# Where the residual input of a decoder layer is turned: on TensorE inside the output projection, or by VectorE's block transposes early, kept in DRAM

## The chip, the cores and the metric

The kernel runs on one core of a Trainium2 chip. The metric is the device time of one execution in microseconds (us). Before the change it is 1391.66 us, the median of 3 runs (1391.24 to 1391.66). A single execution was also taken with the hardware profiler; every number of the trace below is from that one.

## The reference

One layer of a hybrid decoder is computed for 1024 prompt tokens and 8 sample tokens, which the kernel treats as one set of 1032 columns. The width is 1024. With the branch details left out:

```python
h = rmsnorm(x, g_attn_norm)
z = h @ w_in                       # q, k, v of both branches, output gate, merge gates
y_a = attention(...) @ w_att_out   # sliding window of 128, sinks
y_m = mlstm(...) @ w_mlstm_out     # chunkwise matrix memory
mixed = sigmoid(gate_a) * y_a + sigmoid(gate_m) * y_m
x = x + mixed @ w_out              # the residual add of this case
h2 = rmsnorm(x, g_ffn_norm)
x = x + (silu(h2 @ w_gate) * (h2 @ w_up)) @ w_down
return rmsnorm(x, g_final)         # and caches and states
```

All arrays are float32. What matters here is the line `x = x + mixed @ w_out`: the raw input `x` is needed a second time, after about two fifths of the work.

## The kernel before, in words

**Layout.** Activations live with the channel on the partition and the token along the row, in 8 blocks of 128 channels by 1032 tokens. The inputs `x_prompt` and `x_sample` are stored token by token, so the residual has to be turned from [token, channel] to [channel, token] before it can be added. Float32 products are made from a high and a low part of each operand (`split`, L230: ScalarE copies the high part, VectorE subtracts to get the low part), three matmuls for each block.

**Two runs over a list of products.** The function `run` (L334) goes through a list of jobs. The first call (L2114) has 69 of them: 4 tiles by 3 column chunks first, and 19 more tiles by 3 chunks: the input projections and the first merge gates. The second call (L2119) has one job for each of the 32 remaining tiles: 16 branch tiles (8 "wm", 8 "wa", matmuls on L1385) and 16 tiles of the output projection (`wo_tile`, L1233, matmuls on L1261). The output projection makes two passes over the 8 blocks of `w_out`: in the first pass (s = 0) for one half of the tokens, in the second (s = 1) for the other. Between the two calls the other merge gates are computed (`gates`), and after the second the feed-forward part follows.

Within a job: `before()`, the matmuls (with a step of queued side work every few matmuls), the split of the weights that are used two jobs later and the load of those used four jobs later (`next_split`, L340), the evacuation, and `after()`.

**Orders.** The instructions of TensorE, SyncE (SP) and GpSimd are kept in the order in which the program writes them. For VectorE and ScalarE, those written through `main_line` (L287) keep their order among each other. All loads and most stores are issued from SP's queue, one behind the other; a transfer whose buffer is not free yet holds up all those that are written after it. Small tiles come from a pool of 11 buffers (`T`, L109), whole activations from one of 20 (`U`, L106).

**The weights of the output projection.** In the first pass each block's high and low parts, after the split, are also stored to DRAM (`KeptSlice`, L190, 512 KB each), and in the second pass loaded from there (`AgainSlice`, L205), so they are split only once.

**The residual.** `xr_load` (L1175) loads a quarter of the channels for all tokens in rows of 1 KB; two quarters are issued in the last branch jobs (L1372), two from the residual's own steps. `residual` (L1187) is side work of the output projection's first pass. For each of 8 channel blocks it transposes 8 token blocks of 128 x 128 and one of 8 tokens on TensorE (L1197, L1202) into a PSUM tile, and ScalarE copies the pieces into `X[s, th, k // 4]` (L1199, L1203), the tiles to which the evacuation adds the product (`add_half`, L1265). Side work of the same pass also splits the mixed activations of the second pass (`mix_rest`, L1218).

Of the kernel before, what the change touches and what calls it, by code (L numbers as in the profile page):

```python
# [11 lines left out]
F32 = mybir.dt.float32  # L12
# [8 lines left out]
P = 128  # L21
D = 1024
NP = 1024
NS = 8
# [19 lines left out]
LAST = (4, 5)  # L44
WARM = (22, 3, 3, 4)
START = 4
PER_A = 2.95
AHEAD = 3
LEAD = 4
# [35 lines left out]
def decoder_step(ctx, tc, x_prompt, x_sample, cache_k, cache_v, st_c, st_n, st_m, rel_bias, w_in, b_if, sinks,  # L85
# [248 lines left out]
    def run(tiles, jobs, sl, loads, splits):  # L334
        last = {}
        for n, (t, c) in enumerate(jobs):
            last[t] = n
        started = set()

        def next_split():  # L340
            main_line(splits.pop(0).split)
            if loads:
                loads.pop(0).load()

        for n, (t, c) in enumerate(jobs):
            tile_ = tiles[t]
            if t not in started:
                started.add(t)
                if tile_.before:
                    tile_.before()  # L350
            if tile_.pre:
                tile_.pre(c)
            rate = tile_.per / sum(len(rhs) for _, rhs in tile_.prods)

            def tick():
                acc[0] += rate
                if acc[0] >= 1.0 - 1e-9:
                    acc[0] -= 1.0
                    side.step(1)

            pss = []
            for i, (w, rhs) in enumerate(tile_.prods):
                if tile_.mm:
                    ps = tile_.mm(w, tick)
                else:
                    ps = ps_g(f"{w.name}_{c}")
                    gemm(ps, w.w, rhs, slice(*CHUNKS[c]), tick)
                pss.append(ps)
                if last[t] == n and splits and not w.own and not tile_.evac_first:
                    next_split()  # L370
            main_line(tile_.evac, c, *pss)
            if last[t] == n and splits and tile_.evac_first:
                next_split()
            if tile_.after:
                tile_.after()
            if n + 2 < FIRST and len(sl) > FIRST and not mark:
                sl[n + 2].split()
            if n + 1 == START and not mark:
                mark.append(len(nc.cur_bb.bb.instructions))

    def call(f, *a):
        f(*a)
        yield

    def rstd(v):
        dve.tensor_scalar(v, v, 1.0 / D, EPS, op0=ALU.mult, op1=ALU.add)
# [774 lines left out]
    X = {}  # L1161
    XG = {}
    mixed = {}
    xr = {}
    ssq = {}
    pools = {}
    R = {}
# [4 lines left out]
    def ps_d(name):  # L1172
        return pools["pd"].tile([P, 2, 512], F32, tag="d", name=name)

    def xr_load(q):  # L1175
        cols_ = slice(q * 256, (q + 1) * 256)
        for i in range(0, NB, 2):
            t = T(f"xr{i}_{q}", [P, 2, 256])
            sp.dma_start(t, x_prompt[0, i * P:(i + 2) * P, cols_].rearrange("(u p) d -> p u d", p=P))
            xr[q, i], xr[q, i + 1] = t[:, 0], t[:, 1]  # L1180
        t = T(f"xr{NB}_{q}", [P, 256])
        sp.dma_start(t[0:NS, :], x_tok[NB][:, cols_])
        xr[q, NB] = t

    PIECES = ((0, ((0, 0, 258), (1, 258, 512))), (4, ((1, 512, 516), (2, 516, 774), (3, 774, 1024))))

    def residual():  # L1187
        for k in range(KD):
            if k % 4 == 0:
                for s in range(2):  # L1190
                    for th in range(2):
                        X[s, th, k // 4] = U(f"x1_{s}{th}{k // 4}", shape=[P, 4, HB])
            q, o = k // 2, k % 2 * P
            for b0, pieces in PIECES:
                tps = ps_t(f"xr{b0}_{k}")
                for j in range(4):
                    pe.transpose(tps[:, j * P:(j + 1) * P], xr[q, b0 + j][:, o:o + P], ident)  # L1197
                for c, a, b in pieces:
                    act.copy(X[c % 2, c // 2, k // 4][:, k % 4, a - c * HB:b - c * HB], tps[:, a - b0 * P:b - b0 * P])  # L1199
                yield  # L1200
            tps = ps_t(f"xr{NB}_{k}")
            pe.transpose(tps[:, 0:NS], xr[q, NB][0:NS, o:o + P], ident[0:NS, 0:NS])  # L1202
            act.copy(X[1, 1, k // 4][:, k % 4, HB - NS:HB], tps[:, 0:NS])  # L1203
            if k in (1, 3):
                xr_load(q + 2)
            yield

    def mix_split(s, th, ks):
        for kh in range(2):
# [8 lines left out]
    def mix_rest():  # L1218
        for th in range(2):
            for k in range(0, KD, 2):  # L1220
                main_line(mix_split, 1, th, range(k, k + 2))
                yield

    d_x1 = [dp.tile([P, NT], F32, name=f"d_x1_{j}") for j in range(KD)]

    def wo_start():
        res = residual()
        side.add(itertools.islice(res, 6), mix_rest(), res)

    stage3 = ExitStack()  # L1230
    kept = {}
# [1 line left out]
    def wo_tile(s, j):  # L1233
# [5 lines left out]
        def before():  # L1239
            if s == 0 and j == 0:  # L1240
                wo_start()
                side.step(2)
            if s == 1 and j == 0:
                side.drain()
            if s == 1 and j == 1:
# [116 lines left out]
    def branch_tile(n, j):  # L1362
# [3 lines left out]
        def before():  # L1366
            if n == "m":
                mixm[j] = U(f"mixm{j}")
                if j == 0:
                    reload(back_a, d_yat, V, "yb")  # L1370
            sg_load(i + 2)
            if n == "a" and j in (5, 6):  # L1372
                xr_load(j - 5)

        def mm(w_, tick):
            rhs = ym if n == "m" else ya
# [891 lines left out]
```

## Time and profile before

| what | value |
|---|---|
| median of 3 runs | 1391.66 us |
| the profiled execution's own time | 1391.65 us |
| its span, from the first to the last instruction | 1389.9 us |
| TensorE busy | 1369.4 us, 99% of the span |
| VectorE, ScalarE, GpSimd busy | 975.4, 617.0, 242.0 us |
| mean granted TensorE clock | 0.997 |
| read from and written to DRAM | 140.31 MB, 68.96 MB |

A line of the trace names the line of the kernel, the engine, the operation, and the tiles as output<-input. "PE" is TensorE, "PEld" its weight load, "DVE" VectorE, "ACT" ScalarE, "POOL" GpSimd, "SPq" the queue that SyncE feeds. Matmuls overlap, so the time from the start of one to the start of the next is shorter than the duration shown. The DMA share of a stretch is the mean busy share of the core's 16 DMA engines.

### The profile page before, as it was taken

The page shows a single profiled execution, that of the slowest core. Times are in us where ns is not written, and L with a number is a line of the kernel's source. Part 1 is how long each engine was busy: PE and PEld are TensorE (multiplying, and loading weights), DVE is VectorE, ACT ScalarE, POOL GpSimd, SP SyncE. Part 2 cuts the span into 40 slices and gives each one's busy share as a digit, 9 for nine tenths or more (in the row PEclk, how much of TensorE's full clock was granted, in tenths as well). Part 3 has the DMA queues.
Part 4 walks back from the last instruction along what each step waited for, and adds up shares of the span by engine and source line. Part 5 has one row for each costly group of instructions (what it writes and reads, how often), then busy time and mean ns, then how long its engine had stood idle before and what let it go on. Part 6 is the DMA issues. An engine that isn't in the chain of part 4 may idle for free.

```text
span 1389.9 us, 26966 instructions
## 1 busy us (share of the span) xinstructions
PE 1369.4 (99%) x10723; PEld 1337.9 (96%) x10724; DVE 975.4 (70%) x1853; ACT 617.0 (44%) x1407; POOL 242.0 (17%) x303
## 2 busy tenths in 40 slices
PE   9999999999999999999999999999999999999996
PEld 7999889999999999999999999999999999999996
DVE  7252758886944444755587888898888878888875
ACT  6243567654443331374454343444433343333325
POOL 4012111001111100001132232333333220000003
PEclk9999999999999999999999999999999999999998
DMA  7144224114233274788423344544434468677633
GB/s 224 32 117 113 62 63 100 31 62 149 81 107 100 84 283 137 221 281 283 166 77 120 110 153 153 168 168 139 131 114 144 146 214 304 220 239 237 221 123 122
DMA packets 179173, 208.42 MB, mean 150 GB/s; under 512 B 20638, under 2 KB 137634, under 8 KB 179032
## 3 DMA queue, kind: packets, MB, share of 16 engines
q1 hardware_dynamic: 161928, 151.72, 35.1%
q0 software_dynamic: 16688, 54.40, 10.7%
q8 instruction: 84, 1.38, 0.4%
q10 hardware_dynamic: 432, 0.59, 0.1%
q14 instruction: 41, 0.34, 0.1%
HBM read 140.31 MB, written 68.96 MB: 151 GB/s over the span
## 4 chain that ended last, share of the span: by engine, by line
PE 90%; DVE 3%; ACT 2%; DMA 2%; issue 1%; POOL 0%; SPq 0%; ACTq 0%; POOLq 0%; DVEq 0%
PE af L1589 18%; PE df L1589 9%; PE ad L1589 7%; PE wo L1261 6%; PE bf L1589 5%; PE ag L1589 4%; PE dd L1589 4%; PE o L226 3%; PE mv L226 3%; PE wm L1385 3%; PE wa L1385 3%; PE q L226 3%; PE dg L1589 2%; PE bd L1589 2%; PE mk L226 2%; PE gm L226 2%
## 5 line engine op out<-in xcount | busy, mean ns | idle before, releaser
L125 POOL TENSOR_TENSOR s1f<-s1f,R 128x516 f32<-128x516 f32 x42 | 68.8, 1637 | 87.2 <-DVE s1f L125 71.5
L1589 PE MATMUL df<-Th,op6f 128*128 128x258 f32 x352 | 67.3, 283 | 1.3 <-DVE uu L125 1.3
L1589 PE MATMUL af<-Th,op0f 128*128 128x258 f32 x352 | 67.4, 284 | 0.0
L1589 PE MATMUL bf<-Th,op2f 128*128 128x258 f32 x352 | 67.3, 283 | 0.0
L1589 PE MATMUL df<-Th,op4f 128*128 128x258 f32 x352 | 67.3, 284 | 0.0
L1589 PE MATMUL af<-Th,op1f 128*128 128x258 f32 x352 | 67.1, 283 | 0.0
L1589 PE MATMUL af<-Th,op3f 128*128 128x258 f32 x352 | 66.9, 283 | 0.0
L1589 PE MATMUL af<-Th,op5f 128*128 128x258 f32 x336 | 64.1, 283 | 0.0
L1625 ACT ACTIVATE s1f<-s1f 128x516 f32<-128x516 f32 (+1 forms) x23 | 14.2, 618 | 103.5 <-POOL s1f L125 103.5
L1589 PEld LDWEIGHTS df<-Th,op6f 128*128 128x128 f32 x352 | 55.9, 189 | 1.5 <-DVE uu L125 1.5
L1589 PEld LDWEIGHTS af<-Th,op1f 128*128 128x128 f32 x352 | 56.0, 189 | 0.0
L1589 PEld LDWEIGHTS af<-Th,op0f 128*128 128x128 f32 x352 | 56.0, 189 | 0.0
L1589 PEld LDWEIGHTS bf<-Th,op2f 128*128 128x128 f32 x352 | 56.0, 189 | 0.0
L1589 PEld LDWEIGHTS df<-Th,op4f 128*128 128x128 f32 x352 | 55.8, 189 | 0.0
L1589 PEld LDWEIGHTS af<-Th,op3f 128*128 128x128 f32 x352 | 55.6, 189 | 0.0
L1589 PEld LDWEIGHTS af<-Th,op5f 128*128 128x128 f32 x336 | 53.4, 190 | 0.0
L125 POOL TENSOR_TENSOR s2f<-s2f,R 128x516 f32<-128x516 f32 x21 | 27.4, 1307 | 135.5 <-ACT s2f L1625 135.4
L1589 PE MATMUL bf<-Tl,op2f 128*128 128x258 f32 x176 | 49.8, 283 | 0.0
L1589 PE MATMUL df<-Tl,op6f 128*128 128x258 f32 x176 | 49.7, 282 | 0.0
L1589 PE MATMUL af<-Tl,op1f 128*128 128x258 f32 x176 | 49.7, 282 | 0.0
L1589 PE MATMUL af<-Tl,op0f 128*128 128x258 f32 x176 | 49.7, 282 | 0.0
L1589 PE MATMUL df<-Tl,op4f 128*128 128x258 f32 x176 | 49.7, 282 | 0.0
(690 smaller groups left out, 4935.9 us busy)
## 6 DMA issues: line engine op xcount, KB each, us to landing
ta<-d_t SPq DMA_DIRECT2D x63, 516.0 KB, 6.6
Yd<-in_w_down_dram SPq DMA_DIRECT2D x40, 256.0 KB, 3.5
d_t<-h POOLq DMA_DIRECT2D x18, 516.0 KB, 5.2
d_t<-t POOLq DMA_DIRECT2D x18, 516.0 KB, 4.6
Xf<-in_w_gate_dram SPq DMA_DIRECT2D x22, 256.0 KB, 4.1
Xf<-in_w_up_dram SPq DMA_DIRECT2D x22, 256.0 KB, 6.9
Yf<-in_w_gate_dram SPq DMA_DIRECT2D x22, 256.0 KB, 3.0
Yf<-in_w_up_dram SPq DMA_DIRECT2D x22, 256.0 KB
```

The costliest lines, as they stand in the source:

```text
L125: return eng.tensor_tensor(out=out, in0=a, in1=b, op=op)
L226: pe.matmul(o, a[:, k, :], b[:, cs], start=(k == 0 and i == 0), stop=(k == n - 1 and i == len(passes) - 1))
L1261: pe.matmul(ps[:, th, 0:HB], a[:, k, :], b, start=(k == 0 and i == 0), stop=(k == KD - 1 and i == 2))
L1385: pe.matmul(ps[:, c, 0:CW], a[:, k, :], b[:, cs], start=(k == 0 and q == 0), stop=(k == 3 and q == 2))
L1589: pe.matmul(ps[:, s if ps.shape[1] > 1 else 0, 0:HB], a, b, start=(first and k == 0 and i == 0), stop=(k == self.nk - 1 and i == 2), skip_ ...
L1625: act.activation(s, s, AF.Silu)
```

## The change

The transposes on TensorE and the copies on ScalarE go. In their place, `turn_step` is called behind the jobs of `run`. There are 16 units of one channel block by 512 tokens, and one for the sample tokens. A unit is loaded by four DMAs on SP's queue so that each partition holds, for 16 groups of 32 tokens, one run of 32 channels (128 bytes); one VectorE instruction transposes each block of 32 x 32 in place of a full transpose; one DMA on SP's queue stores the result to a DRAM array `d_xT` in [channel, token] order. Load, transpose and store of a unit lie one step apart each. There is a step behind two of every three jobs, from job 6 on, in a run with more than 30 jobs.

In the output projection, `x_again` loads the tiles `X` from `d_xT`: four tiles of 516 KB before the first product, four more as side work after `mix_rest`. `mix_rest` now takes two steps of side work for each pair of blocks.

```diff
+TURN = 6
@@ run
             if tile_.after:
                 tile_.after()
+            if len(jobs) > 30 and n >= TURN and n % 3 != 2:
+                turn_step((n - TURN) // 3 * 2 + (n - TURN) % 3)
...
+    d_xT = dp.tile([P, KD, NT], F32, name="d_xT")
+    units = [(k, a) for a in (0, 512) for k in range(KD)] + [None]
+    turned = {}
+
+    def turn_load(n):
+        if units[n] is None:
+            t = T("xs_in", [P, 256])
+            pool.memset(t, 0.0)
+            for q in range(4):
+                sp.dma_start(t[32 * q:32 * q + NS, :].rearrange("j (k i) -> j k i", i=32),
+                             x_tok[NB].rearrange("j (k q i) -> q j k i", q=4, i=32)[q])
+        else:
+            k, a = units[n]
+            t = T(f"xi{k}_{a}", [P, 512])
+            for q in range(4):
+                c = k * P + 32 * q
+                sp.dma_start(t[32 * q:32 * q + 32, :].rearrange("j (m i) -> j m i", i=32),
+                             x_prompt[0, a:a + 512, c:c + 32].rearrange("(m j) i -> j m i", j=32))
+        turned[n] = t
+
+    def turn(n):
+        t = turned[n]
+        o = T(f"xo{n}", list(t.shape))
+        dve.transpose(out=o, in_=t)
+        turned[n] = o
+
+    def turn_store(n):
+        o = turned.pop(n)
+        if units[n] is None:
+            sp.dma_start(d_xT[:, :, NP:NT], o.rearrange("p (k j) -> p k j", j=32)[:, :, 0:NS])
+        else:
+            k, a = units[n]
+            sp.dma_start(d_xT[:, k, a:a + 512], o)
+
+    def turn_step(n):
+        for f, lag in ((turn_store, 2), (turn, 1), (turn_load, 0)):
+            if 0 <= n - lag < len(units):
+                main_line(f, n - lag)
...
-    def xr_load(q):
-    def residual():
+    def x_again(kh):
+        for s in range(2):
+            for th in range(2):
+                X[s, th, kh] = U(f"x1_{s}{th}{kh}", shape=[P, 4, HB])
+                sp.dma_start(X[s, th, kh], d_xT[:, 4 * kh:4 * kh + 4, cols_of(s, th)])
...
     def mix_rest():
                 main_line(mix_split, 1, th, range(k, k + 2))
                 yield
+                yield
...
     def wo_start():
-        res = residual()
-        side.add(itertools.islice(res, 6), mix_rest(), res)
+        x_again(0)
+        side.add(mix_rest(), call(x_again, 1))
...
             if s == 0 and j == 0:
                 wo_start()
-                side.step(2)
...
-            if n == "a" and j in (5, 6):
-                xr_load(j - 5)
```

More of the change, by code (lines that the diff above doesn't have):

```diff
@@ L1163, in decoder_step @@
     mixed = {}
-    xr = {}
     ssq = {}
@@ L1173, in ps_d @@
         return pools["pd"].tile([P, 2, 512], F32, tag="d", name=name)
-    def xr_load(q):
[L1176 to L1185, printed above, removed]
-    def residual():
[L1188 to L1206, printed above, removed]
+    def x_again(kh):
[3 more added lines that the diff above has]
+                sp.dma_start(X[s, th, kh], d_xT[:, 4 * kh:4 * kh + 4, cols_of(s, th)])
     def mix_split(s, th, ks):
```

## The prediction

> **What bounds the kernel now.** I read the page's busy times first, then the windows of the stages that the change touches, the groups of the lines concerned, the DMA issues and SP's waits, and last the timeline of SP's queue.
>
> ```profile
> span 1389.9 us, 26966 instructions
> PE 1369.4 (99%) x10723; PEld 1337.9 (96%) x10724; DVE 975.4 (70%) x1853; ACT 617.0 (44%) x1407; POOL 242.0 (17%) x303
> ```
>
> TensorE has work for 99% of the span, so an instruction taken from it is worth its full time as long as nothing else becomes late. The next view cuts the span at the start of the output projection's first pass (587.7), of its second (644.5) and at its end; the first row is the early projections. The columns are the length, the busy times, the granted clock, the DMA share and GB/s.
>
> ```profile
> 35.00:165.00 130.00, 130.00 (x884) 123.69 (x883) 53.15 (x132) 52.54 (x125) 18.33 (x30) 1.00 0.31 80
> 531.00:587.70 56.70, 56.70 (x363) 56.70 (x362) 34.52 (x59) 12.73 (x25) 0.00 (x0) 1.00 0.59 187
> 587.70:644.50 56.80, 56.28 (x458) 54.77 (x457) 28.16 (x63) 35.63 (x109) 0.00 (x0) 1.00 0.86 279
> 644.50:692.60 48.10, 48.10 (x403) 47.49 (x403) 31.40 (x59) 21.69 (x45) 9.17 (x10) 1.00 0.61 208
> ```
>
> TensorE is never free for long, the clock is full, and VectorE has room everywhere. The DMA engines do not: in the first pass of the output projection they are busy for 0.86 of the time. That stretch holds the transposes that go, and it gets the new loads.
>
> **The change part by part.**
>
> *What TensorE loses.* The groups of the residual's transposes and of the output projection's matmuls (count, shortest/median/longest, first and last start):
>
> ```profile
> L1197 PE MATMUL xr<-cst,xr x64: 270/273/294, 587.8 to 625.3; 128*128 128x128 f32 x64
> L1202 PE MATMUL xr<-cst,xr x8: 223/223/225, 589.5 to 626.2; 8*128 8x8 f32 x8
> L1199 ACT COPY x<-xr x40: 136/374/415, 588.4 to 625.9; 128x258 f32<-128x258 f32 x16, 128x254 f32<-128x254 f32 x8, 128x4 f32<-128x4 f32 x8, 128x250 f32<-128x250 f32 x8
> L1203 ACT COPY x<-xr x8: 147/172/202, 590.0 to 626.5; 128x8 f32<-128x8 f32 x8
> L1261 PE MATMUL wo<-mh,wl_wo0b x16: 278/282/292, 644.6 to 650.0; 128*128 128x258 f32 x16
> L1261 PE MATMUL wo<-mh,wl_wo4b x16: 279/282/293, 672.0 to 677.4; 128*128 128x258 f32 x16
> L1261 PE MATMUL wo<-mh,wl_wo5b x16: 278/282/292, 677.7 to 683.1; 128*128 128x258 f32 x16
> ```
>
> The durations overlap, so I take the difference of two passes. A product without transposes goes from 672.0 to 677.7, 5.7 us; eight are 45.6. The first pass takes 56.8 with its 72 transposes, so 11.2 us go if nothing holds the matmuls up (10.7 if the 0.5 us of idle time in that row, 56.80 less 56.28, stays). ScalarE's 48 copies go too; with 35.63 of 56.80 us busy it sets nothing, and I count nothing.
>
> *What comes in, and how often.* The call of `turn_step` asks for a run of more than 30 jobs. The first run has 69. The second has one job for each remaining tile: 8 + 8 branch tiles and 8 + 8 output projection tiles, 32. That is more than 30, so by the code the same units are loaded, turned and stored a second time, from job 6 of the second run (the seventh branch tile) to its last. Nobody needs it, since `d_xT` is full by then. Jobs 6 to 15 (branch) get 7 loads and 5 stores, jobs 16 to 23 (first pass) 5 and 5, jobs 24 to 31 (second pass) 4 and 6, and the sample unit's load.
>
> *Price of a load.* No row shows packets of 128 bytes. A unit has 512 tokens x 4 runs, 2048 packets. The nearest row is a load in 256-byte packets (113 to 118 us); beside it one in 512-byte packets (98 to 101.5). The columns are packets, MB, and share of the 16 engines.
>
> ```profile
> q1 hardware_dynamic: 2118, 0.54, 52.0%
> q1 hardware_dynamic: 843, 0.43, 49.8%
> ```
>
> The first is 0.520 x 5 us x 16 / 2118 = 19.6 ns a packet, the second 0.498 x 3.5 x 16 / 843 = 33 ns. Through both, 128 bytes come to 13 ns, and a unit to 2048 x 13 / 16 = 1.7 us of all engines. Not below what its 262 KB need at 405 GB/s, a high rate shown below, 0.65 us; above, at the 256-byte price, 2.5. I take 1.7. A DMA takes SP some 0.4 us to issue (rows below), so a full step about 2 us of a 5.7 us job.
>
> The Trainium skill, "DMA: Bandwidth & Descriptors", section "Specifications", asks for at least 512 bytes a transfer for full rate, below which the engine reads, modifies and writes. The 256-byte row shows no such penalty, as its packets are cheaper than those of 512 and not dearer; no run here shows 128. By that rule the sum would be rival B's instead of mine.
>
> *VectorE.* A one-operand instruction on 128x512 takes 684 ns:
>
> ```profile
> L889 DVE COPY apt<-at x16: 660/684/692, 228.7 to 326.2; 128x512 f32<-128x512 f32 x16
> ```
>
> No row shows a block transpose; at half of this or twice of it, five in the first pass are 1.7 to 6.8 us, where VectorE is idle for 28 of 56.8. As arithmetic they are free; without that cover 17 would be 11.6. But they stand in VectorE's written order, so one whose load is late holds the next split and evacuation. I take 1 us for it, 0 to 3.
>
> *First run.* 17 units in the stretch from 35 to 165: 16 x 1.7 = 27 us of loads and 4.2 MB of stores (12) beside a share of 0.31. That fits. But SP's queue is not free there:
>
> ```profile
> SPq L472 <- DVE rowe L471: 35.1, 1, 35.1
> 92.64 0.29 SPq L472 DMA_DIRECT2D out_dram<-rowe  x1
> 93.03 0.37 SPq L168 DMA_DIRECT2D ws_mv<-in_w_in_dram  x1
> 98.64 0.37 SPq L168 DMA_DIRECT2D ws_k<-in_w_in_dram  x1
> ```
>
> A small store waits until 92.6 and holds all that is written behind it, now turning loads too. A transpose whose load sits there waits on VectorE ahead of the next split, and the loads then issue ahead of weights whose split is two jobs away. 0 to 6 us; I take 1.5, since each slice of weights lasts three jobs here.
>
> *Branch stretch.* 0.59 of 56.7 is 33.5 us; less 2 MB of residual loads (6.5), plus 7 x 1.7 and 5 stores (4), 43 of 56.7. No loss.
>
> *First pass of the output projection.* What is moved there now, by queue issues in that window, is
>
> ```profile
> DMA packets 13949, 15.86 MB, mean 279 GB/s; under 512 B 686, under 2 KB 11879, under 8 KB 13943
> d_wo<-wh_wo SPq DMA_DIRECT2D x7, 512.0 KB, 3.6
> ws_wo<-in_w_out_dram SPq DMA_DIRECT2D x5, 512.0 KB, 6.4
> xr<-in_x_prompt_dram SPq DMA_DIRECT2D x8, 256.0 KB, 5.7
> d_x<-x SPq DMA_DIRECT2D x11, 129.0 KB, 5.8
> ```
>
> Take away 8 x 262 KB of residual loads, add 8 tiles of 516 KB from `x_again` and 5 turned stores of 262 KB: 15.86 - 2.1 + 4.2 + 1.3 = 19.3 MB. The rate is 279 / 0.86 = 324 GB/s while busy; two pressed microseconds at the upper end are
>
> ```profile
> 584.00:586.00 2.00, 2.00 (x15) 2.00 (x14) 1.97 (x4) 0.00 (x0) 0.00 (x0) 1.00 1.07 405
> ```
>
> I take 340, nearer the stretch's own, as the mix is the same: 56.8 us, and 5 x 1.7 = 8.5 for the loads, 65.3 in a pass that TensorE could do in 45.6. That is 19.7 over. Not all of it has to land in the pass: the second batch of `d_x` stores and the first weights of the feed-forward part, 2.1 MB, may be 6 us late. The rest must not, because the queue is served in order and the second pass's weights are loaded through it. How tight that is already:
>
> ```profile
> 592.12 0.32 SPq L190 DMA_DIRECT2D d_wo<-wh_wo  x1
> 592.92 0.32 SPq L190 DMA_DIRECT2D d_wo<-wl_wo  x1
> 593.29 0.46 SPq L168 DMA_DIRECT2D ws_wo<-in_w_out_dram  x1
> 593.80 3.42 SPq L1179 DMA_DIRECT2D xr<-in_x_prompt_dram  x4
> 598.10 0.76 DVE L125 TENSOR_TENSOR x<-wo,x 128x258 f32<-128x258 f32 x2
> wh_wo1b<-d_wo SPq DMA_DIRECT2D x1, 512.0 KB, 7.9
> 642.05 0.43 SPq L205 DMA_DIRECT2D wl_wo1b<-d_wo  x1
> L1261 PE MATMUL wo<-mh,wl_wo1b x16: 278/287/387, 650.3 to 658.2; 128*128 128x258 f32 x16
> ```
>
> The second block's weights are issued by 642.05, take some 7.9 us, and are used at 650.3: no slack. The start has the same trouble: `x_again` is written behind that split's stores and the unit loaded at job 15, so its 2 MB are issued from about 594, behind 1.5 MB (4.6 us at 340 GB/s), and the first two tiles (3.1) land near 602, where the evacuation now runs at 598.1; three PSUM buffers carry TensorE that far, not much further. So about 19.7 - 6 = 13.7 us of waiting on TensorE. Ends: at 405 GB/s and 0.65 a unit 47.6 + 3.3 - 45.6 - 6, nothing; at 324 and 2.5 with nothing held over 59.5 + 12.5 - 45.6, 26.
>
> *Second pass.* 208 GB/s x 48.1 = 10.0 MB, 6 stores 1.6 MB: 34 us at 340, with 4 x 1.7 and 6 us carried in 47, in 48. Full on average, so a burst makes it wait: 3, from 0 to 10.
>
> *Sum.* -11.2 + 13.7 + 3 + 1.5 + 1 = +8.0. The profiled execution took 1391.65 us (the span of 1389.9 and 1.75 around it), as good as the median of the runs shown, 1391.66. So 1399.7.
>
> **The rivals.**
>
> *A: the queue takes it.* For it: the 405 row, and 8 us of the first pass (0.14 of 56.8) without transfers. Against it: the second block's weights, just in time at 650.3. At 405 GB/s the first pass waits 47.6 + 8.5 - 45.6 - 6 = 4.5 at 1.7 us a unit and nothing at 0.65; I take 2, and for the second pass, the first run and VectorE 1 + 1 + 0.5: -11.2 + 4.5 = -6.7, 1385. With these small other terms it decides from about 372 GB/s up (51.8 + 8.5 - 51.6 = 8.7, which cancels the gain).
>
> *B: the short packets are dear.* If 128-byte packets cost twice the 256-byte ones, 39 ns, a unit is 5.0 us: 5 x 3.3 = 16.5 more in the first pass, about 10 more in the second, 5 in the first run: 8 + 31.5, about 1431. No row speaks for it; against it, packets fall from 33 to 19.6 ns as they halve. It decides from about 30 ns a packet up (3.8 us a unit, 10 more in the first pass). It is what the Trainium skill's rule above would do ("DMA: Bandwidth & Descriptors", "Specifications").
>
> *C: the second turning does not take place* (it does what its description says, once). The code speaks against it. Then the first pass needs 18.0 MB, 53 us, 1.4 over after the 6 held: -11.2 + 1.4 + 1.5 + 0.5, 1384.
>
> **How the numbers follow.** The forecast's case, with a wait that outweighs the gain by more than the 0.2% (2.8 us) that a measurement tells from none, 0.55; its own range is +3 to +24. A 0.23, B 0.09, C 0.04, and 0.09 that gain and wait cancel. Faster 0.27, same 0.09, slower 0.64. The range takes most of A in below and stops short of B: 1382 to 1417 (about 0.08 of the chance lies below, 0.11 above).
>
> **What would show it.** Two sets of block transposes on VectorE, 17 by about 165 us and 17 between 530 and 700, with 33 stores to `d_xT`. First pass from wo to wo0b: 45 to 50 us means A or C, 58 to 62 the forecast, over 70 B. DMA share there above 0.95, with ScalarE or VectorE waiting on `ws_wo`, `x` or `xi`, or TensorE on wo0b and wo1b. Landing times of `xi` give the packet price. I am wrong if the second set is missing, if the first pass shortens by 8 us or more, or if the loss lies in the early stretch.

## The result

The changed kernel takes 1426.24 us (median; 1425.06 to 1429.47 over 4 runs) beside 1391.45 us of the kernel before on the same chip (1390.88 to 1391.66 over 4). The ratio is 1.0253, 95% interval 1.0238 to 1.0268: 34.8 us slower, where 8.0 were forecast and 1417 was the upper end of the range. Line numbers from here on are those of the changed kernel: the projections' matmuls stand on L227, those of the output projection on L1276, the transposes on L412, the units' loads on L405, their stores on L421, the store of the row maxima on L515.

The page's first lines, then the groups of the transposes and the transfers that are new (count, size, median us to landing):

```profile
span 1423.0 us, 27056 instructions
PE 1373.1 (96%) x10651; PEld 1341.0 (94%) x10652; DVE 994.5 (70%) x1887; ACT 606.4 (43%) x1359; POOL 238.6 (17%) x305
```

```profile
L412 DVE STREAM_TRANSPOSE xo<-xi x32: 689/704/712, 39.3 to 722.7; 128x512 f32<-128x512 f32 x32
L412 DVE STREAM_TRANSPOSE xo<-xs_in x2: 423/431/439, 172.8 to 729.7; 128x256 f32<-128x256 f32 x2
...
xi<-in_x_prompt_dram SPq DMA_DIRECT2D x128, 64.0 KB, 3.6
d_xT<-xo SPq DMA_DIRECT2D x32, 256.0 KB, 4.5
x<-d_xT SPq DMA_DIRECT2D x8, 516.0 KB, 7.9
```

Both turnings take place: 34 transposes, 128 + 8 loads, 33 stores. A transpose takes 0.70 us. TensorE's share of the span falls from 99% to 96%; its waits are new. The view of what TensorE waited for (total, times, longest), and with it the largest of VectorE's and SP's waits that concern the change:

```profile
PE wo L1276 <- DVE wl_wo L126: 9.9, 2, 5.7
PE wo L1276 <- DMA wl_wo0b<-d_wo: 8.5, 1, 8.5
PE mv L227 <- DVE wl_mv L126: 5.5, 1, 5.5
PE mu L638 <- DVE bmb L126: 2.4, 1, 2.4
...
DVE xo L412 <- DMA xi<-in_x_prompt_dram: 43.8, 9, 11.8
...
SPq L515 <- DVE rowe L514: 23.5, 1, 23.5
```

Where the time went is read from the first start of each stage's matmuls (from the groups of each tile). All stages are laid side by side with the runs that follow; "x to y" is the time between the two starts. The stages of a row are those of its one profiled execution. That lies within 0.7 us of the median in every row but two: e15's took 1392.7 us, the slowest of its ten, and e17's 1391.3, the fastest of its ten.

| kernel | median | mv to q | q to gm | ga to wo | first pass | wo0b to wo5b | wo5b to last stage |
|---|---|---|---|---|---|---|---|
| before | 1391.5 | 87.7 | 165.6 | 248.2 | 56.0 | 33.1 | 669.5 |
| changed | 1426.2 | 97.0 | 168.2 | 247.3 | 69.9 | 38.0 | 672.7 |
| e1 early turning added to before | 1405.4 | 97.2 | 169.0 | 248.2 | 56.1 | 33.1 | 670.3 |
| e12 early loads added to before | 1399.3 | 91.7 | 168.4 | 248.1 | 56.1 | 33.2 | 670.3 |
| e2 turning once | 1404.2 | 96.8 | 168.6 | 247.4 | 53.9 | 33.9 | 670.2 |
| e8 second time only loads | 1420.4 | 97.4 | 168.4 | 247.3 | 67.6 | 35.7 | 671.0 |
| e4 both times, long rows | 1414.8 | 93.9 | 168.2 | 247.3 | 64.4 | 37.3 | 671.6 |
| e17 once, a third of the jobs | 1396.4 | 87.7 | 168.3 | 247.6 | 52.9 | 33.6 | 669.4 |
| e15 between the runs, half rate | 1389.5 | 87.7 | 168.0 | 249.3 | 47.0 | 38.4 | 669.8 |
| e18 the same, last tiles later | 1385.0 | 87.7 | 165.4 | 249.0 | 47.0 | 34.4 | 669.5 |

"ga to wo" of the kernel before, e1 and e12 ends with 0.8 us of the residual's transposes, which start at 587.8 us, ahead of the first product at 588.6; a kernel without them that loses nothing there shows 247.3 to 247.6.

In the changed kernel the first run loses 9.3 us up to the start of q and 2.6 up to gm, the branch stretch nothing, the first pass of the output projection 13.9, the second with the start of the feed-forward part 8.1.

The windows of the first two losses (length, busy times, granted clock, DMA share, GB/s). Of the kernel before:

```profile
99.00:110.00 11.00, 11.00 (x74) 10.78 (x73) 1.95 (x10) 3.40 (x9) 3.19 (x6) 1.00 0.72 170
110.00:122.00 12.00, 12.00 (x78) 12.00 (x77) 1.29 (x2) 2.41 (x5) 0.00 (x0) 1.00 0.30 67
588.60:644.60 56.00, 55.48 (x451) 53.98 (x450) 27.26 (x62) 35.45 (x109) 0.00 (x0) 1.00 0.85 279
```

Of the changed kernel:

```profile
99.00:110.00 11.00, 5.88 (x27) 5.64 (x28) 2.60 (x4) 2.19 (x7) 3.19 (x6) 0.69 0.89 198
110.00:122.00 12.00, 12.00 (x78) 12.00 (x77) 3.16 (x12) 2.41 (x5) 0.00 (x0) 1.00 0.74 167
...
599.60:669.50 69.90, 51.27 (x386) 50.43 (x385) 34.31 (x73) 27.89 (x66) 0.00 (x0) 0.87 0.93 283
669.50:679.70 10.20, 8.43 (x48) 8.26 (x48) 8.09 (x10) 3.30 (x6) 0.00 (x0) 0.72 1.03 284
```

Two things are to be seen. TensorE is idle for 18.6 us of the first pass. And the clock stands at 0.69 and 0.87: a stall costs more than its length. The timeline of TensorE round the first stall (start, us, operation, idle before it), and further below two-microsecond windows round one in the first pass:

```profile
98.29 0.32 PE L227 MATMUL mv<-hh,wh_mv 128*128 128x344 f32 x1
104.12 0.62 PE L227 MATMUL mv<-hh,wl_mv 128*128 128x344 f32 x1 [5.51 <-DVE wl_mv L126]
104.54 0.49 PE L227 MATMUL mv<-hl,wh_mv 128*128 128x344 f32 x1
104.83 0.49 PE L227 MATMUL mv<-hh,wh_mv 128*128 128x344 f32 x1
...
109.47 0.32 PE L227 MATMUL mv<-hl,wh_mv 128*128 128x344 f32 x1
109.63 0.32 PE L227 MATMUL mv<-hh,wh_mv 128*128 128x344 f32 x1
```

VectorE's timeline shows why `wl_mv` was late: a transpose waits for its unit, and the split of the weights stands behind it in VectorE's order.

```profile
102.69 0.71 DVE L412 STREAM_TRANSPOSE xo<-xi 128x512 f32<-128x512 f32 x1 [4.32 <-DMA xi<-in_x_prompt_dram]
103.33 1.25 DVE L126 TENSOR_TENSOR wl_mv<-ws_mv,wh_mv 128x512 fp32r<-128x512 f32 x2
```

The windows in the first pass:

```profile
618.00:620.00 2.00, 0.00 (x0) 0.00 (x0) 1.42 (x4) 1.83 (x6) 0.00 (x0) 1.00 0.92 224
620.00:622.00 2.00, 0.00 (x0) 0.00 (x0) 2.00 (x7) 1.87 (x5) 0.00 (x0) 0.64 1.04 391
622.00:624.00 2.00, 1.87 (x8) 1.87 (x9) 1.78 (x5) 0.95 (x3) 0.00 (x0) 0.50 1.04 388
624.00:626.00 2.00, 2.00 (x12) 2.00 (x11) 1.50 (x5) 1.85 (x7) 0.00 (x0) 0.50 1.16 326
626.00:628.00 2.00, 2.00 (x13) 2.00 (x13) 1.74 (x5) 1.12 (x2) 0.00 (x0) 0.66 1.13 278
```

After the first stall the starts lie 0.29 us apart in place of 0.16, from 104.1 to about 109.2: 5.1 us at half pace, so some 2.5 us beside the 5.5 of the wait itself. The second stall shows the same, 0.50 until about 627. In the run that turns once (e2 below), a wait of 1.9 us left the clock at 1.00:

```profile
616.00:620.00 4.00, 2.12 (x18) 1.91 (x17) 2.89 (x8) 3.67 (x10) 0.00 (x0) 1.00 1.05 378
```

The Trainium skill, "TensorE: Matmul & The Clock Gate", section "Why this matters for your kernels", advises against gaps of more than about 3 us between bursts of matmuls, for this reason. The trace agrees in the main: the mean of 0.64 over 620 to 622 us puts the fall at about 620.6, 2.6 us after the idle time began. But the runs draw no sharp line: a single wait of 2.40 us in e12 (to 129.5 us) was followed by a clock of 0.50 until about 132.2, and one of 2.66 us in e2 (to 653.8 us) left the clock at 1.00.

### The profile page after: what moved, and what is told of

Its sections match the earlier page's. It is cut to its first block, busy times and chain, and to the rows that moved or that the text cites. A ratio compares the mean times of both kernels' runs of the same rounds, so it can differ in the third digit from the quotient of the medians.

```text
span 1423.0 us, 27056 instructions
## 1 busy us (share of the span) xinstructions
PE 1373.1 (96%) x10651; PEld 1341.0 (94%) x10652; DVE 994.5 (70%) x1887; ACT 606.4 (43%) x1359; POOL 238.6 (17%) x305
## 3 DMA queue, kind: packets, MB, share of 16 engines
q0 software_dynamic: 16688, 54.40, 10.4%
## 4 chain that ended last, share of the span: by engine, by line
PE 74%; DMA 4%; DVE 3%; SPq 3%; ACT 2%; issue 1%; POOL 1%; POOLq 0%; ACTq 0%; DVEq 0%
PE af L1602 17%; PE df L1602 9%; PE ad L1602 7%; PE bf L1602 4%; PE ag L1602 4%; PE dd L1602 4%; PE o L227 3%; PE wm L1398 3%; PE wa L1398 3%; PE dg L1602 2%; PE q L227 2%; PE wo L1276 2%; PE bd L1602 2%; PE gm L227 2%; PE ga L227 1%
## 5 line engine op out<-in xcount | busy, mean ns | idle before, releaser
L1602 PE MATMUL af<-Th,op3f 128*128 128x258 f32 x352 | 67.6, 284 | 0.0
L412 DVE STREAM_TRANSPOSE xo<-xi 128x512 f32<-128x512 f32 x32 | 22.6, 705 | 44.0 <-DMA xi<-in_x_prompt_dram 43.8
L1602 PE MATMUL af<-Tl,op3f 128*128 128x258 f32 x176 | 49.8, 283 | 0.0
```

The costliest lines, as they stand in the source:

```text
L412: dve.transpose(out=o, in_=t)
L1602: pe.matmul(ps[:, s if ps.shape[1] > 1 else 0, 0:HB], a, b, start=(first and k == 0 and i == 0), stop=(k == self.nk - 1 and i == 2), skip_ ...
```

## The experiments

Each was timed beside runs of the kernel before on the same chip. The experiments were spread over several chips, on which the medians of the kernel before were 1391.3 to 1391.8 us. Ratios are to it, with their 95% interval.

**Which part loses what (e1, e2, e8).** e1 is the kernel before with `turn_step` in the first run alone and the residual as it was. e2 is the changed kernel with one number changed:

```diff
-            if len(jobs) > 30 and n >= TURN and n % 3 != 2:
+            if len(jobs) > 40 and n >= TURN and n % 3 != 2:
```

e8 turns as before the first time, and the second time only loads:

```diff
-        for f, lag in ((turn_store, 2), (turn, 1), (turn_load, 0)):
+        for f, lag in ((turn_store, 2), (turn, 1), (turn_load, 0))[2 * again:]:
```

> The kernel before, with the turning added in the first run alone; nothing reads the turned copy, the residual is made as before. Theory (in the first run the turning loads stand behind the small store of the row maxima on SP's queue, VectorE's written order waits for them, the weight split behind is late, and TensorE's clock is halved for some us after the idle): the first run's 12 us alone, 1403 (1401 to 1406), with the same idle stretch of 4 to 6 us on TensorE near 99 us. Rival (the first run's loss is small as I predicted, and the later stages cost the rest): 1391 to 1394.

> The changed kernel with the condition len(jobs) > 40, so that the second run turns nothing. Theory (the useless second turning overloads the queue and holds VectorE in the output projection; a load in 128-byte packets is not dear in itself): the first run's 12 us stay, the output projection's first pass falls from 69.9 us to 48 to 52, the second has no wait: 1391.4 + 12 - 7 = 1396 (1392 to 1400). Rival (the 4.2 MB that the output projection loads back are enough to overload it, with or without a second turning): 1415 or more.

> The changed kernel, but in the second run the 17 units are only loaded, neither transposed nor stored again. Against the run that turns once it adds the loads alone, against the changed kernel it leaves out VectorE's waits for them and the stores of 4.2 MB. Theory by bytes and packets (2.2 us of all engines for a unit, 10 units in the two passes): 22 us of DMA time, of which the first pass's half shows in full, 1404 + 11 to 15 = 1417 (1413 to 1420). Rival (what costs is VectorE, held at a transpose ahead of a split, and not the transfers): 1404 to 1408.

e1: 1405.44, ratio 1.0101 (1.0085 to 1.0116). The first run's loss stands by itself, 13.8 us. e2: 1404.19, 1.0091 (1.0076 to 1.0107), so the second turning costs 22 us, but without it the output projection gains next to nothing: its first pass takes 53.9 us, not the 48 to 52 expected. e8: 1420.39, 1.0207 (1.0192 to 1.0222): 16 of those 22 us are the loads alone (the time is 0.4 us above the range expected). The pass windows of e2, then of e8:

```profile
599.90:653.80 53.90, 47.21 (x386) 46.40 (x384) 29.98 (x66) 27.42 (x66) 0.00 (x0) 1.00 0.95 318
```

```profile
600.20:667.80 67.60, 50.39 (x386) 49.39 (x385) 35.52 (x71) 29.61 (x68) 0.00 (x0) 0.92 0.93 272
```

The first pass can now be added up: 45.6 of matmuls, 8.3 that stay in e2, 13.7 for the second loads, 2.3 for their transposes and stores: 69.9. Six units are loaded in this pass and not five, as SP's queue is late (24 issues, four a unit, in e8 as in the changed kernel), so a unit's load costs 2.3 us.

**Short packets or the number of transfers (e4, e16).** e4 loads each unit of the changed kernel, e16 of the kernel that turns once, in rows of 2 KB; e16 in one transfer in place of four. The units then hold another part of the input, so the residual that is added is another one. The diff is that of e16:

```diff
-            for q in range(4):
-                c = k * P + 32 * q
-                sp.dma_start(t[32 * q:32 * q + 32, :].rearrange("j (m i) -> j m i", i=32),
-                             x_prompt[0, a:a + 512, c:c + 32].rearrange("(m j) i -> j m i", j=32))
+            sp.dma_start(t, x_prompt[0, k * P:k * P + P, a:a + 512])
```

> The changed kernel, both turnings, each unit of 256 KB loaded in rows of 2 KB in place of 2048 runs of 128 bytes; it then holds another part of the input, so the residual that is added is another one. Same number of transfers, transposes and stores. Theory (17 ns for a packet, 2.2 us of all engines for a unit, against about 0.8 us in long rows): 1.4 us x 5 units less in the first pass, up to 4 us less in the second, nothing in the first run, where a held load is late however long it is: 1415 (1410 to 1422). Rival (the short packets are what costs): 1397 or less. Rival (the number of transfers and VectorE's order alone decide): 1424 to 1428.

> As the run that turns once, each unit loaded by one transfer of 128 rows of 2 KB in place of four transfers of 512 runs of 128 bytes; it holds another part of the input, so the residual that is added is another one. The run with four transfers of rows lost 8.8 us by the start of gm where the changed kernel lost 12. Theory (number of issues): three issues less, 1.6 us of SP a unit, the first run loses 2 to 6 us, 1397 (1394 to 1400). Rival (packets only): 1400 to 1402, as with four transfers of rows. Rival (neither): 1404.

e4: 1414.78, 1.0173 (1.0154 to 1.0192), as expected: the first pass is 5.5 us shorter, 0.9 us for each of its six units. The first run is 3.1 us shorter, where nothing was expected. The packets are a third of the loss, not the cause of it. e16: 1404.25, 1.0088 (1.0073 to 1.0103), the same as e2. It gains 2.0 us by q and loses 4.3 between q and gm, which stays unexplained. That SP's number of issues is the cause has no support here.

**What holds the first run (e3, e6, e12, e13).** e3 issues the held store elsewhere; e6 puts a step more between load and transpose; e12 adds the loads alone to the kernel before; e13 issues the units' loads and stores from ScalarE's queue (`act.dma_start` in `turn_load` and `turn_store`).

```diff
-        sp.dma_start(p_m[0, 0, :].rearrange("(h o) -> h o", o=1), mr[h4, NP - 1:NP])
+        pool.dma_start(p_m[0, 0, :].rearrange("(h o) -> h o", o=1), mr[h4, NP - 1:NP])
```

```diff
-        for f, lag in ((turn_store, 2), (turn, 1), (turn_load, 0)):
+        for f, lag in ((turn_store, 3), (turn, 2), (turn_load, 0)):
```

```diff
-        for f, lag in ((turn_store, 2), (turn, 1), (turn_load, 0)):
+        for f, lag in ((turn_load, 0),):
```

> As the run that turns once, with the small store of the row maxima (p_m) issued from GpSimd's queue in place of SP's. Theory (that store is what holds the turning loads): 8 to 11 us less than the run that turns once, 1386 (1383 to 1390), and no idle stretch of TensorE near 99 us. Rival (VectorE's own time for the transposes, or the shared small buffers, make the first run late): within 2 us of the run that turns once.

> As the run that turns once, with one step (about 5.7 us in that stretch) more between a unit's load and its transpose. Revised theory: the waits of VectorE for a load of 4 to 6 us are covered, the longest of 11.8 us half of it: 5 to 9 us less than the run that turns once, 1397 (1394 to 1401). Rival (loads and splits hold each other through SP's queue, so that one more unit under way only moves the wait): 1402 or more.

> The kernel before with the first run's 17 unit loads alone, nothing transposed or stored. Theory (VectorE's written order, waiting for the loads, is what made the first run late): most of the 13.8 us gone, 1394 (1391 to 1397), no idle stretch of TensorE near 99 us. Rival (SP's queue is full of issues after the held store, so weights and rows come late with or without transposes): 1400 or more.

> As the run that turns once (1404, turning in the first run), with the units' loads and stores issued from ScalarE's queue in place of SP's. Theory (a unit takes SP five issues, about 3 us, in a step of 5.7, and its loads stand behind SP's waits, so VectorE waits for them): the first run's 12 us fall to 1 to 6, 1396 (1392 to 1399). Rival (the loads are late because of the transfers themselves, or the transposes make VectorE late): 1402 or more. ScalarE's own time for the issues is a cost that no run has shown yet.

e3: 1414.12, 1.0162 (1.0145 to 1.0179), ten us worse than e2 where ten less were expected. The held store is not the cause; it had even kept the units clear of something worse. The transfers on the units' tile between 76 and 95 us, and what waited:

```profile
L405 SPq DMA_DIRECT2D xi<-in_x_prompt_dram x8: 366/634/7622, 79.3 to 92.9; - x8
...
DVE xo L412 <- DMA xi<-in_x_prompt_dram: 38.8, 5, 14.0
...
PE mv L227 <- ACT mv L1047: 11.0, 1, 11.0
```

Not all loads and stores go through SP's queue, as the description of the kernel before has it: GpSimd's queue moves 54.4 MB there. One issue took SP 7.6 us, in the time in which a 1.5 MB transfer of GpSimd's queue (`d_b<-d_t`, issued at 75.7, 14.0 us to landing) was under way, and VectorE stood 14.0 us at the transpose. Behind it stood the gate rows, behind them ScalarE, which empties TensorE's accumulators.

e6: 1404.29, 1.0086 (1.0071 to 1.0101), no change. The wait for `wl_mv` shrinks to 0.8 us, and 6.2 us come back near 130 us, where TensorE waits for ScalarE and that for VectorE, which waited 10.2 us for a unit. The rival was right: the wait only moves.

e12: 1399.32, 1.0056 (1.0041 to 1.0071), between theory and rival. The idle near 99 us is gone, and so are 6 of the 13.8 us: that much is VectorE's order with the stores. The other 8 need no transpose at all: 4.0 of them lie by the start of q, 2.8 between q and gm, 0.8 in the last stages. Its windows:

```profile
99.00:110.00 11.00, 11.00 (x74) 10.78 (x73) 1.95 (x10) 3.56 (x9) 3.17 (x6) 1.00 0.96 151
110.00:122.00 12.00, 12.00 (x78) 12.00 (x77) 1.29 (x2) 2.42 (x5) 0.00 (x0) 1.00 0.70 157
122.00:130.00 8.00, 5.60 (x42) 4.96 (x41) 4.68 (x12) 6.06 (x17) 0.29 (x1) 0.96 1.05 166
130.00:140.00 10.00, 10.00 (x68) 9.28 (x67) 2.42 (x10) 2.60 (x6) 5.08 (x10) 0.86 1.05 210
```

The DMA engines are busy for 0.70 to 1.05 of the time from 99 to 140 us: SP issues 11 of the 17 units between 93 and 135 us, once the store has let it go, beside the weights and the rows of the matrix memory.

e13: 1407.99, 1.0113 (1.0098 to 1.0128), 4 us worse than e2. The Trainium skill, "DMA: Bandwidth & Descriptors", section "Issuing engines are not separate DMA queues", says that another issuing engine saves only the time of issuing. The run agrees as far as it goes: VectorE waited 34.0 us for units, in e2 28.6 (from the groups of the units' tiles). An issue took ScalarE 0.50 us in the median, which is ScalarE's own time.

**Small buffers (e5, e11).** e5 turns once, with `TURN = 36`. e11 is the kernel before with the pool `tp` at 7 buffers in place of 11.

> As the run that turns once, with TURN = 36: the same 17 units in the first run, from its job 36 on (about 190 us) in place of job 6. Revised theory (VectorE comes in its written order to a transpose one step after its load is written; between 57 and 140 us the load is late, first behind the store of the row maxima, and without that behind a 1.5 MB transfer of GpSimd's queue and behind weight loads that wait for VectorE's own splits; after 190 us the DMA share is 0.1 to 0.4 and nothing holds SP): the first run costs 0 to 3 us, so 11 us less than the run that turns once, 1393 (1390 to 1397). Rival (17 transposes, 34 transfers and two more small buffers cost some 12 us wherever they stand in the first run): 1400 or more.

> The kernel before with 7 small buffers in place of 11, no turning: what is left to the others when two units' inputs and two outputs are under way. Theory (the late turning lost 22 us between 163 and 351 us because its units took these buffers from the attention's and the states' tiles): 5 to 20 us slower, between the starts of q and gm, 1397 to 1411. Rival (the transfers and transposes were what cost there, buffers are plenty): 1391 to 1393.

e5: 1414.12, 1.0154 (1.0137 to 1.0171), ten us worse than e2 although the DMA share is only 0.29 to 0.64 there (190 to 320 us): my theory of the place fell. Nothing is lost by q (163.4), but 22.3 us between q and gm. SP's waits name something else:

```profile
SPq L405 <- PE at L928: 18.1, 3, 10.3
...
SPq L405 <- PE ay L948: 14.7, 4, 5.3
```

A unit's load waits for a small buffer that attention still reads, and holds SP's queue meanwhile. e11: 1454.39, 1.045 (1.0433 to 1.0468), far more than the 5 to 20 us expected. Most of its 63 us lie behind the first run; in it, 0.6 us are lost from mv to q, but 9.6 from q to gm. So buffers are short in the stretch where e5 put its units, and not where the changed kernel loses its 9.3 us. Where its 2.6 us between q and gm come from stays open: the profiled execution of e15, which turns nothing there, has 2.4 of them too, and that of e18, whose first run is the same as e15's, has none.

**Another place, another rate (e9, e10, e14, e15, e17).** e9 turns between the two runs, one step ahead of each product of the merge gates; e10 adds a later `x_again` (below); e14 is e10 with ScalarE's queue; e15 is e10 with a step ahead of every second product; e17 is e2 with a step behind every third job. The first diff is that of e15; in e9, e10 and e14 every product has its `turn_step(next(count))`, and a transpose follows two steps behind its load. e15 has one step between them, about as long as two of e10 (some 7 us), and begins at the third product in place of the sixth.

```diff
         def step(v, n, sets, hk_):
+            m = next(count)
+            if m % 2 == 0:
+                turn_step(m // 2)
             v.product(n, sets)
```

```diff
-            if len(jobs) > 40 and n >= TURN and n % 3 != 2:
-                turn_step((n - TURN) // 3 * 2 + (n - TURN) % 3)
+            if len(jobs) > 40 and n >= TURN and n % 3 == 0:
+                turn_step((n - TURN) // 3)
```

> As the run that turns once, but the turning is taken out of the first run and put between the two runs: one step ahead of each product of the remaining merge gates from the sixth on (from about 365 us; two steps of some 4.3 us between load and transpose). There the DMA share is 0.25 to 0.46, VectorE is busy for less than half and no attention or state work needs the small buffers. Theory (the first run's loss is a matter of place: SP's held queue, VectorE's order and the shared small buffers there): first run as before, merge gates 0 to 1 us longer, so 12 us less than the run that turns once, 1391 (1388 to 1394). Rival (a load in 128-byte runs, a transpose and a store per unit cost what they cost, wherever they stand): 1400 or more.

> As the run with the turning between the two runs, with the second half of the tokens loaded back only at the end of the first pass of the output projection and in the second, and the first two tiles written ahead of the last branch tile's product. Theory (the first pass waits for tiles that stand behind the split's stores, and is bound by the DMA engines): 2 to 5 us less than the run with the turning between the runs, 1387 (1385 to 1390), below the kernel before. Rival (the two passes together are bound by the bytes, so the waits come back in the second): within 1.5 us of it.

> As the run with the turning between the two runs and half of the tiles loaded back later (1397.6), with the units' loads and stores issued from ScalarE's queue. Theory (SP's issues fill a step there: 3.3 us of 3.5): the 8.3 us that the merge gates lost fall to 0 to 3, 1391 (1388 to 1394). Rival (transfers or VectorE): 1396 or more.

> As the run with the turning between the two runs and half of the tiles loaded back later (1397.6), on SP's queue, but with a step ahead of every second product only (some 7 us a step, one step between load, transpose and store). Theory (SP's issue rate is what binds): the merge gates lose 0 to 3 us in place of 8.3, 1391 (1388 to 1394). Rival (each unit costs its half us wherever it stands): within 1.5 us of 1397.6.

> As the run that turns once (1404), in the first run from job 6, with a step behind every third job in place of two of three: about 11 us a step in the projections, and the units reach to about 320 us. Theory by rate (nine units, held or spread over 93 to 140 us, fill the DMA engines to 0.7 to 1.05 there, and VectorE, the rows of the matrix memory and the weights come late; half as many do not): the 9.5 us that are lost by the start of q fall to 0 to 4; but units are then under way between 190 and 320 us, where the run with 7 small buffers lost 9.6 us, so 3 to 9 come back there: 1399 (1395 to 1404). Rival (the held store alone, 26 us of SP at one place, decides, at any rate): the loss by the start of q stays at 8 to 10, 1404 or more.

e9: 1400.07, 1.0066 (1.0051 to 1.0081). The first run is as before to a tenth of a microsecond, but the merge gates lose 10.4 us (ga to wo 258.6, in a profiled execution 3.1 us above the median): the loss moved with the turning. e10: 1397.63, 1.0045 (1.003 to 1.006), 256.5. e14: 1405.32, 1.0095 (1.0078 to 1.0111), worse again. e15: 1389.47 over ten runs, 0.9983 (0.9974 to 0.9992): with half the rate the gates lose 1.1 us in place of 8.3, in the same stage, with the same loads, transposes and stores, but spread further: the units are loaded from 347 to 454 us in place of 379 to 430. (Against the 247.4 of e2, which has no transposes there either, each of these losses is 0.8 larger.) VectorE's wait for units in e10, and in e15, where the transpose stands on L410:

```profile
DVE xo L410 <- DMA xi<-in_x_prompt_dram: 18.9, 13, 3.2
```

```profile
DVE xo L410 <- DMA xi<-in_x_prompt_dram: 12.1, 6, 3.7
```

TensorE's idle time between 341 and 470 us falls with it, from 7.4 us to 2.4 us (from 343):

```profile
340.80:470.00 129.20, 121.85 (x920) 120.18 (x919) 83.90 (x114) 50.43 (x92) 16.26 (x31) 0.99 0.64 170
```

```profile
342.80:470.00 127.20, 124.79 (x964) 123.71 (x963) 86.70 (x120) 52.70 (x95) 17.44 (x33) 1.00 0.67 175
```

e17: 1396.38, 1.0033 (1.0021 to 1.0044), 8 us less than e2. Its profiled execution is the fastest of its ten (1391.28; the others to 1400.20), so its trace shows the best case, and where the other 5.1 us of the median lie is not known: q at 163.4, nothing lost by then, with the store of the row maxima where it was and the clock at 1.00:

```profile
99.00:110.00 11.00, 11.00 (x74) 10.78 (x74) 3.37 (x12) 3.43 (x9) 3.19 (x6) 1.00 0.85 186
122.00:130.00 8.00, 8.00 (x59) 7.29 (x57) 4.44 (x11) 5.82 (x15) 2.61 (x5) 1.00 0.43 104
```

**The load back (e7, e18).** e7 is e2 with the tiles of the second half of the tokens loaded at the end of the first pass and at the start of the second; e10 and e15 have this too, with the first two tiles written ahead of the last branch tile's product. e18 is e15 with the last two tiles two blocks later; the diff is that of e18, and in the others the last line stands behind `side.drain()`.

```diff
+            if s == 0 and j == 7:
+                x_again(0, (1,))
             if s == 1 and j == 0:
                 side.drain()
+            if s == 1 and j == 2:
+                x_again(1, (1,))
```

> As the run that turns once, but in the output projection only the four tiles of the first half of the tokens are loaded back in the first pass (two ahead of it, two as the first side work), those of the second half at the last tile of the first pass and the start of the second: 2.1 MB leave the first pass (at 324 to 350 GB/s 6 us). Theory (the 4.1 MB loaded back, 2.1 more than the residual's loads in that pass before, keep the first pass bound by the DMA engines, at a share of 1.07 over most of 608 to 640 us): 4 to 7 us less than the run that turns once, 1399 (1396 to 1401). Rival (the bytes come back as waits in the second pass, or the first pass is bound by the order on VectorE): 1403 or more.

> As the run with a step ahead of every second product of the merge gates (1389.5), with the last two tiles loaded back two blocks later in the second pass, behind the weights of the third and fourth block. Theory (that pass still waits 1.9 us for the third block's weights, which stand behind two of these tiles on SP's queue): 1 to 3 us less, 1388 (1386 to 1390). Rival (the pass is bound by the transfers before it, so the wait only moves): within 0.7 us of it.

e7: 1402.35, 1.0075 (1.006 to 1.009), between theory and rival. The first pass gains 3.3 us (50.6), the second loses 2.8. With the first tiles ahead of the queue's other work as well, e15's first pass takes 47.0. e18: 1385.02 over five runs, 0.995 (0.9936 to 0.9963), 4.4 us less than e15, more than expected. Its two passes (590 to 637, 637 to 672):

```profile
590.00:637.00 47.00, 46.60 (x386) 46.39 (x386) 27.87 (x64) 25.55 (x62) 0.00 (x0) 1.00 1.02 338
637.00:672.00 35.00, 34.01 (x283) 33.23 (x283) 22.88 (x42) 15.32 (x31) 6.03 (x10) 1.00 0.81 270
```

This version is faster than both kernels: 6.7 us below the one before, with the turning done once, at half the rate, between the runs, and the load back spread over both passes.

## Why the prediction was wrong

The direction was right, the time 26.5 us too low. The terms for the first run and for the first pass are each more than 10 us too low, that for the second pass 5. One of the signs of being wrong that I gave came true in part: 12 of the 34.8 us lie in the early stretch. Step by step:

- **What TensorE loses, -11.2 us: right in kind, 1.4 too much.** The same matmuls without transposes take 47.0 us in e15 and e18, 9.0 less than in the kernel before, and 0.8 of transposes ahead of the first product are gone too: 9.8. The eight products take 46.6 us of busy time in e18, and not 45.6.
- **Twice, not once: right**, and it is the larger part of the loss, 22 us (e2 against the changed kernel).
- **Price of a unit, 1.7 us (0.65 to 2.5): right.** From 68.5 to 71 us only the short packets of one unit's load are under way, over 67 to 73 us also the store of another unit, 128 packets of 2 KB (packets, MB, share of the 16 engines; the longer stretch first). The short ones alone give 0.595 x 2.5 us x 16 / 1865 = 12.8 ns a packet and 1.6 us a unit, where the line through two rows gave 13 ns. The longer stretch gives a mean of 17.2 ns over both kinds; the 17 ns and the 2.2 us a unit in the expectations of e4 and e8 are that mean, and too high for the load. Where three units' loads stand one behind the other (e12, 61 to 63 and 62 to 64 us), 2369 and 1983 short packets pass in 2 us, 13.5 and 16.1 ns of each engine's time for one. The 2.3 us a unit in the first pass is therefore not the packets' price alone: it holds what a late load delays.

```profile
q1 hardware_dynamic: 2256, 0.52, 40.4%
q1 hardware_dynamic: 1865, 0.23, 59.5%
```

- **The first run, 1.5 us (0 to 6): this is the step that failed.** It measured 12, 13.8 alone in e1. I added the loads to a share of 0.31 over 130 us and wrote "That fits", and I took little for the waits because each slice of weights lasts three jobs. That cushion did not hold: the split of `wl_mv` began at 103.3 us behind a late transpose, and TensorE had stood since 98.6. The store, which I had seen, holds SP for 23.5 us and then pushes the loads into a stretch where the kernel before already had 0.72 (99 to 110 us). There the units arrive late, VectorE's order makes splits and gate rows late (6 us by e12), and the loads alone cost 8. Which of store, order and full engines comes first can't be separated to the microsecond: each was moved by itself (e3, e6, e13, e16), and the loss stayed or grew. What removed it by q was fewer units in the same time: in the first run in the one execution of e17 that was profiled, and between the runs in e15. That the rate alone did it is not shown, since both also spread the units over a longer stretch.
- **First pass, 13.7 us of waiting (0 to 26): the mechanism was right, the size off.** It measured 24.3 beside the 45.6 of matmuls. On TensorE, 18.6 of these are idle time, 4.7 are the slow clock after it, for which I had no term (busy for 51.3 us, the same matmuls in e18 for 46.6), and 1.0 is what 45.6 was short. On the DMA engines the work was right: 65.3 us were forecast, and a share of 0.93 over 69.9 is 65.0. e2 moves 17.1 MB in its pass of 53.9 us (18.0 were counted), 318 GB/s, or 335 in the 0.95 of the time in which its engines were busy; 340 was assumed. What failed are the 6 us that I let be held over: they did not come off, and the next pass's first weights were 8.5 us late instead. Without that credit the pass would have been put at 65.3, 4.6 short, about as long as its DMA engines were not busy (4.9).
- **VectorE, 1 us (0 to 3): in its range for the first pass** (2.3 with the stores, e8), too low over both passes (5.8 with the stores, the changed kernel less e8), and wrong for the first run, for the reason above.
- **Second pass, 3 us (0 to 10): low**, 8.1 with the start of the feed-forward part; 1.8 of it is TensorE's idle time at 669.5 to 679.7, where the clock stands at 0.72 (0.50 until about 675.2).
- **The branch stretch, no loss: right** (247.3 us for 248.2, of which 0.8 were transposes).

The rivals: A needed 372 GB/s, and the full pass of e2 moved 318, 335 while its engines were busy. B asked for 39 ns a packet; 12.8 were measured, and long rows give back 11.5 of 34.8 us. The first pass's length alone would not have told B from the forecast: 69.9 us lie above the 58 to 62 named for the forecast and next to the 70 named for B. C is e2 as a run: 1384 was forecast for it and 1404 came, 10.6 us of that by the first run (12.1 for 1.5) and 6.9 by the first pass, which I had put at 47.0.

## What to carry to other kernels

Work that is spread over a stream of jobs should be costed at the place where it collects, behind each wait of the queue that issues it, and not against the mean of a long stretch. Work in another engine's written order needs its inputs early even when it is a small share of that engine's time: here, halving the rate and spreading the units brought 8 us, in the first run (e17) as between the runs (e15), where another queue, one transfer for four in longer packets or one more step of lead brought nothing (e13, e14, e16, e6). And a stall of TensorE should be counted with the slow clock that may follow it: here 1.3 us behind a wait of 2.4 us (e12), and 1.8 to 2.8 us each behind waits of 4.2 to 8.5 us (the changed kernel).

## What the hardware showed that was not expected

- The clock after a stall: 0.50 for 5.1 us after an idle time of 5.5 us, 1.00 throughout after one of 1.9 us. Between these, a wait of 2.40 us brought 0.50 (e12) and one of 2.66 us did not (e2).
- One issue of a 64 KB transfer on SP took 7.6 us (median 0.63 in that stretch) while a 1.5 MB transfer of GpSimd's queue was under way (e3). That the one holds up the other was not tested by itself.
- Moving a stall's cause often moved the stall: five of the runs that took one suspected cause of the first run's loss away (e3, e5, e6, e13, e16) ended at the same time or later.
